# Branch B's meta keys: four heads packed into one transposed block, evacuated onto the diagonal of one operand

## The chip, the cores and the metric

The kernel runs on one core of a Trainium2 chip. The metric is the device time of one execution in microseconds (us); several executions are timed and their median is given. PE is TensorE, DVE is VectorE, ACT is ScalarE, POOL is GpSimd, SP is SyncE, which here issues the DMAs. L12 is line 12 of the kernel. Lines of the kernel before are used unless a text says otherwise.

## The reference

One encoder block on a sequence of 1024 tokens with width 1024, with 16 learned meta tokens set in front: RMS norm, one projection, two attention branches side by side, sigmoid gates, an output product, a SwiGLU feed-forward of width 2816, and a final norm. All in float32. Branch A is differential attention of 4 heads over all keys. Branch B is the one that changes: 8 query heads in 2 key-value groups, head width 64. A block of 128 queries sees the key block before it, its own, the one after it (keys at most 128 away), and always the 16 meta keys, which carry no distance bias. A sink logit joins the softmax's denominator.

```python
kpos = jnp.concatenate([meta_pos, N_META + win_idx], axis=1)
bias = -slopes[None, :, :, None, None] * dist[:, None, None]
s = jnp.einsum('bnqgrd,bnkgd->bngrqk', q, k).astype(jnp.float32) * scale + bias
m = jnp.maximum(jnp.max(s, axis=-1, keepdims=True), sink_b)
p = jnp.exp(s - m)
denom = jnp.sum(p, axis=-1, keepdims=True) + jnp.exp(sink_b - m)
return jnp.einsum('bngrqk,bnkgd->bnqgrd', (p / denom).astype(v.dtype), v)
```

## The kernel before

**Precision.** A float32 factor is split into a high part (ACT copy into the matmul format fp32r) and a low part (DVE or POOL subtracts the high part). A projection sums three products, high times high, high times low and low times high. For P·V in branch B, V's high and low parts lie side by side in the 128 columns of `vb`, and P's two parts are two moving operands.

**Stages.** Tokens are normed and transposed into `hT_hi` and `hT_lo`. Branch B's group 0 is projected and attended while branch A's heads 0 and 1 are projected (L646 to L652); then group 1's queries are projected (L681) and its units run with the projection of branch A's heads 2 and 3 (L693 to L700). Then come the first gate products (L710 to L721) and branch A's attention with more gate products between, the output product and the feed-forward.

**A unit.** `attend_b` (L316) does one tile of 128 queries for the four heads of one group; with 2 groups and 8 tiles there are 16 units. Its first part makes the scores on PE (`bps`, L331), adds the bias and takes the row minimum on DVE (L333), exponentiates on ACT (L337) with the sink beside it (L339), sums and inverts on DVE (L340, L341) and scales the probabilities `bs` on POOL (L343). POOL then copies the 16 meta columns of each head, twice, into `bmd` (L347), of which two zeroed buffers exist (L271 to L274); the two copies are for the high and the low part of the operand. The second part, `finish()`, goes block by block through the two or three key blocks and, as block 8, the meta keys: four transposes per block into one PSUM bank `bpt` (L356, two buffers), an ACT copy to the high part of `btr` (L358), a DVE subtract to the low part (L360; for the meta block only on 16 rows, over the first of its two copies) and the product with V into the bank `bpy` (L362). At the end ACT and DVE add the halves of `bpy` (L365, L366) and SP stores them. `units_b` (L564) keeps at most one unit open behind the one that starts; in group 1 it calls `sums_of` after each first part, which makes weight sums `gs` on POOL (L608 to L611) and stores them (`ws_d`, L613).

**V.** `project_v` (L240) makes V transposed back in three steps, which `project` calls between its matmuls; the last one is the meta tokens, 32 rows, written into block 8 of a `vb` that is zeroed otherwise (L273, L284).

**Order.** On PE, ACT, DVE and SP a scheduler that estimates a timeline sets the order of the instructions (L68); each engine then runs its row in order and waits on semaphores. POOL's row is written by hand from L678 to L726: it is the order of the code. In it, after the last unit, stand the zeroing of `av`, `as` and `dist_m` (L672, L704, L705) with eight copies into `dist_m` (L708), then the low part `wl_c` of the third pair of gate weights (L118, called from L721; those of the first two pairs are made on DVE, L196), then the low parts of the first two operands `w_gop` of the later gate products (L725, L118). `close_bpool` at L694 gives the memory of branch B's tiles away, and `dist_m` lies where some of them were. The first gate products are six banks `pg_0` to `pg_5` of 12 matmuls each (L717), two for each of the three pairs. The loads `w_g` of the operands `w_gop` (L624) go into buffers that weight sums used before.

Of the kernel before, what the change touches and what calls it, by code (L numbers as in the profile page):

```python
# [9 lines left out]
F32 = mybir.dt.float32  # L10
F32R = mybir.dt.float32r
BF16 = mybir.dt.bfloat16  # L12
I32 = mybir.dt.int32
AF = mybir.ActivationFunctionType
ALU = mybir.AluOpType
# [4 lines left out]
P = 128  # L20
S = 1024
D = 1024
NM = 16
L = S + NM
# [49 lines left out]
def encoder_block(ctx: ExitStack, tc: tile.TileContext, x, meta, norm_mix, w_in, lq1, lk1, lq2, lk2,  # L74
                  subln, sink, w_ba, w_bb, w_o, norm_ffn, w_g, w_u, w_d, norm_final, out, dbg=None):
    nc = tc.nc
# [5 lines left out]
    def f32(ap):  # L82
        return ap.bitcast(F32)

    def pool(name, side="left", space=None, bufs=1):
        kw = {} if space is None else {"space": space}
        if space is not DRAM:
            kw["reuse_waits"] = "tile"
        cm = tc.tile_pool(name=name, bufs=bufs, side=side, **kw)
        p = cm.__enter__()  # L90
        return p, lambda: cm.__exit__(None, None, None)
# [5 lines left out]
    def bank(p, tag, name, bufs):  # L97
        return p.tile([P, 512], F32, tag=tag, name=name, bufs=bufs)
# [10 lines left out]
    ident = const.tile([P, P], F32, name="ident")  # L109
# [48 lines left out]
    psum1, close_psum1 = pool("psum1", space=PSUM)  # L158

    def pp_bank(name):  # L160
        return bank(psum1, "pp", name, 3 if psum1 is not psum2 else PP2)
# [58 lines left out]
    def project(col, chunks, name, evac):  # L220
        ensure(1)
        for i, _ in enumerate(project_steps(col, chunks, name, evac)):
            if i % DC == V_AT and turning_v:
                next(turning_v[0], None)
        ensure(W_BUFS - 1)
# [14 lines left out]
    def project_v(col, name, evac):  # L240
        vt = vtpool.tile([P, L + NM], F32, tag="vt", name=f"vt_{name}", bufs=1)
        project(col, K_CHUNKS, name, lambda ps, at, n: nc.scalar.copy(vt[:, at:at + n], ps))
        nc.vector.tensor_copy(vt[:, L:L + NM], vt[:, S:L])

        def turn():
            for b in range(3):
                nb = 4 if b < 2 else 1
                kp = P if b < 2 else 2 * NM
                pt = pp_bank(f"pv_{name}_{b}").rearrange("p (c t) -> p c t", c=4)
                for i in range(nb):  # L250
                    k = 4 * b + i
                    nc.tensor.transpose(pt[:kp, i, :], vt[:, k * P:k * P + kp], ident)
                evac(pt[:kp, :nb, :], 4 * b, nb, kp)
                yield

        turning_v[:] = [turn()]
# [11 lines left out]
    bpool, close_bpool = pool("bpool")  # L268
    kb = [(bpool if g else lowpool).tile([P, 2, NT, 144], F32R, tag=("k1", "kb")[g], name=f"kb{g}", bufs=1) for g in range(BG)]
    vb = [(bpool if g else vtpool).tile([P, 9, P], F32R, tag=("q1", "vb")[g], name=f"vb{g}", bufs=1) for g in range(BG)]  # L270
    mds = [bpool.tile([P, 4, P], F32, name=f"bmd{i}") for i in range(2)]  # L271
    for i in range(2):
        nc.gpsimd.memset(f32(vb[i])[:, 8, :], 0.0)  # L273
        nc.gpsimd.memset(mds[i], 0.0)  # L274

    def kb_consume(st, at, n):
        b0, nb = at // P, n // P
# [38 lines left out]
    def attend_b(g, t, qb):  # L316
        nm = f"{g}_{t}"
        b0, b1 = max(t - 1, 0), min(t + 2, NT)
        nb = b1 - b0
        W = nb * 144  # L320
        j0 = b0 - t + 1
        tb = tbx[:, j0:j0 + nb, :].rearrange("p j k -> p (j k)")
        st = bpool.tile([P, 4, 432], F32, tag="bs", name=f"bs_{nm}", bufs=2)
        mn = small.tile([P, 4], F32, tag="bmn", name=f"bmn_{nm}")
        dn = small.tile([P, 4], F32, tag="bdn", name=f"bdn_{nm}")
        es = small.tile([P, 4], F32, tag="bes", name=f"bes_{nm}")
        hs = slice(4 * g, 4 * g + 4)
        for r in range(4):
            ps = bank(psum1, "bs", f"bps_{nm}_{r}", 2)
            for v in range(2):  # L330
                nc.tensor.matmul(ps[:, :W], qb[:, r, t * P:(t + 1) * P],  # L331
                                 kb[g][:, v, b0:b1, :].rearrange("p b k -> p (b k)"), start=(v == 0), stop=(v == 1))
            nc.vector.tensor_tensor_reduce(st[:, r, :W], ps[:, :W], tb, 2.0 ** -(4 * g + r + 1), nsink[:, 4 * g + r:4 * g + r + 1],  # L333
                                           ALU.add, ALU.min, mn[:, r:r + 1])
        nc.vector.tensor_tensor(es, mn, sinkb[:, hs], ALU.add)
        for r in range(4):
            nc.scalar.activation(st[:, r, :W], st[:, r, :W], AF.Exp, bias=mn[:, r:r + 1], scale=-1.0,  # L337
                                 accum_out=dn[:, r:r + 1])
        nc.scalar.activation(es, es, AF.Exp)  # L339
        nc.vector.tensor_tensor(dn, dn, es, ALU.add)  # L340
        nc.vector.reciprocal(dn, dn)  # L341
        for r in range(4):
            nc.gpsimd.tensor_scalar(st[:, r, :W], st[:, r, :W], dn[:, r:r + 1], 1.0, ALU.mult, ALU.mult)  # L343

        md = mds[t % 2]
        own = (t - b0) * 144 + P
        nc.gpsimd.tensor_copy(md[:, :, 0:2 * NM].rearrange("p r (a k) -> p r a k", a=2),  # L347
                              st[:, :, own:own + NM].unsqueeze(2).broadcast_to([P, 4, 2, NM]))

        def finish():  # L350
            py = bank(psum1, "by", f"bpy_{nm}", 1)
            blocks = [(k, P, (k - b0) * 144) for k in range(b0, b1)] + [(8, P, (t - b0) * 144 + P)]
            for k, kp, o in blocks:
                pt = bank(psum1, "bt", f"bpt_{nm}_{k}", 2).rearrange("p (r t) -> p r t", r=4)
                for r in range(4):
                    nc.tensor.transpose(pt[:kp, r, :], st[:, r, o:o + P] if k < 8 else md[:, r], ident)  # L356
                tr = bpool.tile([P, 2, 4, P], F32R, tag="btr", name=f"btr_{nm}_{k}", bufs=4)
                nc.scalar.activation(tr[:kp, 0], pt[:kp], AF.Copy)  # L358
                lo = tr[:, 1] if k < 8 else tr[:NM, 0]
                nc.vector.tensor_tensor(lo, pt[:lo.shape[0]], f32(tr[:lo.shape[0], 0]), ALU.subtract)  # L360
                for hl in range(2 if k < 8 else 1):
                    nc.tensor.matmul(py, vb[g][:kp, k, :], tr[:kp, hl].rearrange("p r t -> p (r t)"),  # L362
                                     start=(k == b0 and hl == 0), stop=(k == 8))
            y1 = bpool.tile([64, 512], F32, tag="by1", name=f"by1_{nm}", bufs=2)
            nc.scalar.copy(y1, py[64:128])  # L365
            nc.vector.tensor_tensor(y1, py[0:64], y1, ALU.add)  # L366
            nc.sync.dma_start(yb_d[g][:, t * P:(t + 1) * P].rearrange("(r p) s -> p r s", p=64),
                              y1.rearrange("p (r s) -> p r s", r=4))
        return finish
# [130 lines left out]


    first_b = [attend_b(0, t, qb) for t in range(2)]
    project_v(C_VB, "vb", vb_evac)
    flush_v()
    def quad(hl, kh, half):
# [58 lines left out]
    def units_b(g, qb, pending=(), extra=lambda t: None):  # L564
        pending = list(pending)
        for t in range(len(pending), NT):
            if len(pending) > 1:
                pending.pop(0)()
            pending.append(attend_b(g, t, qb))
            extra(t)  # L570
            if len(pending) > 1:
                pending.pop(0)()
        for p in pending:
            p()
# [135 lines left out]
    for k in range(0, 6, 2):  # L710
        ensure(1)
        wh, wl = prepped.pop((k, k + 1))
        for i in range(2):
# [4 lines left out]
            st = f32(stage.tile([P, 2, 512], F32R, tag="qk", name="gate_first", bufs=QK_BUFS))[:, 0]  # L718
# [41 lines left out]
    psum1 = psum2  # L760
# [130 lines left out]
    for n in range(AH * NT + T_LAG):  # L891
        scoring, turning = iter(()), iter(())
        if n < AH * NT:
            h, t = divmod(n, NT)
# [386 lines left out]
    st = {}  # L1281
# [161 lines left out]
    for n in range(nf, len(steps)):  # L1443
        p, j = steps[n][1]
# [3 lines left out]
        if p in LOADS:  # L1448
            at, half, col = LOADS[p]
            if at <= j < at + 4:  # L1450
                t, cols = 4 * half + j - at, slice(col * 512, col * 512 + 512)
# [60 lines left out]
```

## Time and profile before

| | us |
|---|---|
| median of 3 runs | 1451.38 |
| the runs | 1447.25 to 1451.52 |
| the profiled execution | 1446.1 |
| its span (first to last instruction) | 1444.3 |
| PE busy | 1422.8 |
| POOL busy | 641.3 |
| branch B's transposes L356, first and last start | 78.2 and 303.7 |

In a row of a group or a timeline stands the start and the duration (or, in a group, the count and busy time, then the mean of one in ns), the engine, the line, the operation, and output<-inputs with the buffers' numbers left out. A bracket at the end tells how long the engine was idle before and what released it. Matmuls overlap: the duration of one is longer than the distance to the next. In a row of windows stand start and end, the length, the busy time of PE, of its weight loads (PEld), DVE, ACT and POOL, the granted clock of PE, the DMA share and GB/s.

### The profile page before, as it was taken

To read this page: it belongs to the slowest core of one execution; us is meant where nothing else is said; L and a number is where in the kernel's file an instruction comes from. 1 tells how busy PE (TensorE), PEld (TensorE's weight loads), DVE (VectorE), ACT (ScalarE), POOL (GpSimd) and SP (SyncE) were. 2 spreads that over 40 slices of the span, in tenths; PEclk is the share of its full clock that TensorE was granted. 3 is DMA by queue.
4 is the path that set the end of the run, shared out by engine and by line. 5 is a ranking of instruction groups with operands and counts; after the bars stand their busy time and mean duration, and the time that the engine had idled before them with its cause. 6 is when DMAs were issued, how large, how long until landed. Compare 5 with 4: busy or idle time off the path is not lost.

```text
span 1444.3 us, 21160 instructions
## 1 busy us (share of the span) xinstructions
PE 1422.8 (99%) x7279; PEld 1221.2 (85%) x7279; DVE 899.2 (62%) x1624; ACT 679.6 (47%) x1290; POOL 641.3 (44%) x605
## 2 busy tenths in 40 slices
PE   8999999999999999999999999999999999999997
PEld 6988989988898999888888878888888888888886
DVE  7478536637697989624614966554555553787567
ACT  6366535545665656544413643333333333444454
POOL 5599127743333333334522665544544452000444
PEclk9999999999999999999999999999999999999999
DMA  8467658986557473576612534333332332964443
GB/s 244 90 209 237 193 162 265 288 281 213 190 169 257 147 227 125 190 256 209 216 34 88 152 104 161 109 102 110 102 102 96 110 102 102 331 208 140 124 129 139
DMA packets 188891, 242.41 MB, mean 168 GB/s; under 512 B 18208, under 2 KB 115936, under 8 KB 188784
## 3 DMA queue, kind: packets, MB, share of 16 engines
q1 hardware_dynamic: 188784, 241.07, 52.6%
q8 instruction: 57, 0.93, 0.3%
q14 instruction: 50, 0.41, 0.1%
HBM read 157.45 MB, written 77.00 MB: 162 GB/s over the span
## 4 chain that ended last, share of the span: by engine, by line
PE 81%; POOL 6%; DVE 5%; issue 4%; DMA 2%; ACT 1%; POOLq 0%; SPq 0%; DVEq 0%; ACTq 0%
PE pg L1293 28%; PE pd L1387 9%; PE pg L737 7%; PE po L1070 6%; PE ppa L780 6%; PE aps L796 3%; PE pp_qb L214 3%; POOL oa L118 3%; PE apy L835 3%; PE pp_ka L214 2%; PE pp_va L214 2%; PE apt L822 2%; PE pp_qa L214 2%; PE bpt L356 1%; PE bpy L362 1%
## 5 line engine op out<-in xcount | busy, mean ns | idle before, releaser
L118 POOL TENSOR_TENSOR wop<-wf,wop 128x512 fp32r<-128x512 f32 x128 | 172.6, 1353 | 165.5 <-ACT wop L117 149.6
L1293 PE MATMUL pg<-t,wop 128*128 128x512 f32 x1056 | 242.6, 389 | 0.0
L1293 PEld LDWEIGHTS pg<-t,wop 128*128 128x128 f32 x1056 | 198.3, 188 | 41.1
L1387 PE MATMUL pd<-ob,oa 128*128 128x512 f32 x924 | 209.9, 389 | 0.4 <-POOL oa L118 0.4
L1387 PEld LDWEIGHTS pd<-ob,oa 128*128 128x128 f32 x924 | 173.4, 188 | 36.8 <-POOL oa L118 0.8
L1293 PE MATMUL pg<-b,wop 128*128 128x512 f32 x792 | 185.6, 392 | 2.3 <-DVE c L1302 2.3
L1293 PEld LDWEIGHTS pg<-b,wop 128*128 128x128 f32 x792 | 149.5, 189 | 34.1 <-issue 2.4
L737 PE MATMUL pg<-hT_hi,gop 128*128 128x512 f32 x384 | 142.7, 396 | 0.0
L118 POOL TENSOR_TENSOR oa<-ra,oa 128x512 fp32r<-128x512 f32 x33 | 44.0, 1335 | 170.1 <-ACT oa L117 168.6
L117 ACT ACTIVATE wop<-wf 128x512 fp32r<-128x512 f32 x128 | 80.2, 631 | 82.9 <-PE pg L1293 48.6
L118 POOL TENSOR_TENSOR gop<-gr,gop 128x512 fp32r<-128x512 f32 x48 | 63.3, 1319 | 116.4 <-ACT gop L117 102.6
L117 ACT ACTIVATE oa<-ra 128x512 fp32r<-128x512 f32 x77 | 48.7, 632 | 105.9 <-PE pd L1387 45.1
L804 ACT ACTIVATE as<-as,amn 128x1040 f32<-128x1040 f32 x64 | 74.5, 1164 | 46.9 <-DVE amn L799 42.8
L1128 DVE TENSOR_TENSOR s<-wf,wf 128x512 f32<-128x512 f32 x22 | 25.0, 1138 | 108.1 <-DMA wf<-in_w_ff_gate_dram 58.0
L796 PE MATMUL aps<-ak,aq 128*128 128x392 f32 (+1 forms) x384 | 90.0, 330 | 1.3 <-DVE amn L799 0.6
L1070 PE MATMUL po<-woh,mT 128*128 128x512 f32 x384 | 88.0, 390 | 0.0
L1070 PEld LDWEIGHTS po<-woh,mT 128*128 128x128 f32 x384 | 71.9, 188 | 14.8
L796 PEld LDWEIGHTS aps<-ak,aq 128*128 128x128 f32 x384 | 69.6, 189 | 15.0 <-DVE amn L799 2.2
L737 PEld LDWEIGHTS pg<-hT_hi,gop 128*128 128x128 f32 x384 | 72.7, 189 | 11.2 <-DVE gk L742 0.2
L343 POOL TENSOR_SCALAR bs<-bs,bdn 128x432 f32<-128x432 f32 (+1 forms) x64 | 41.4, 666 | 85.5 <-DVE bdn L341 73.4
L737 PE MATMUL pg<-hT_lo,gop 128*128 128x512 f32 x192 | 76.0, 396 | 0.0
L807 POOL TENSOR_SCALAR as<-as,adn,neglam 128x1040 f32<-128x1040 f32 x32 | 38.8, 1214 | 62.5 <-DVE adn L805 43.9
(287 smaller groups left out, 3099.0 us busy)
## 6 DMA issues: line engine op xcount, KB each, us to landing
ra<-aop SPq DMA_DIRECT2D x77, 256.0 KB, 2.6
wf<-in_w_ff_gate_dram SPq DMA_DIRECT2D x24, 512.0 KB, 4.0
wf<-in_w_ff_up_dram SPq DMA_DIRECT2D x24, 512.0 KB, 3.9
aop<-as SPq DMA_DIRECT2D x44, 256.0 KB, 2.1
w_c<-in_w_in_dram SPq DMA_DIRECT2D x17, 512.0 KB, 5.7
aop<-c SPq DMA_DIRECT2D x33, 256.0 KB, 2.0
ts_d<-to SPq DMA_DIRECT2D x16, 512.0 KB, 3.7
gw<-in_w_in_dram SPq DMA_DIRECT2D x32, 256.0 KB, 3.9
```

The source lines that it names most:

```text
L117: nc.scalar.activation(hi, src, AF.Copy)
L118: lo_eng.tensor_tensor(lo, src, f32(hi), ALU.subtract)
L214: nc.tensor.matmul(ps[:, :n], a[:, c, :], b[:, c, at:at + n], start=(c == 0 and i == 0), stop=(c == DC - 1 and i == 2))
L343: nc.gpsimd.tensor_scalar(st[:, r, :W], st[:, r, :W], dn[:, r:r + 1], 1.0, ALU.mult, ALU.mult)
L737: nc.tensor.matmul(ps, op[:, a, c], quad(b, *act)[:, c], start=(p in (2, 5, 1) and c == 0 and i == 0), stop=(p in (2, 3, 4) and c == 3 and ...
L780: nc.tensor.matmul(ps, w[:, a, j, :], src(j, b, tk), start=(j == 0 and n == 0), stop=(j == 3 and n == 2))
L796: nc.tensor.matmul(ps[:, :n], qs[m][:, t * P:(t + 1) * P], ks[m][:, vv, k0:k0 + n], start=(vv == 0), stop=(vv == 1))
L804: nc.scalar.activation(s[m][:, 0:L], s[m][:, 0:L], AF.Exp, bias=low, scale=-1.0, accum_out=dn[:, m:m + 1])
L835: nc.tensor.matmul(py[:, cols], v[:kp, a, k, :], at_[:kp, k, b, :], start=(k == 0 and j == 0), stop=(k == 8))
L1070: nc.tensor.matmul(ps, mT[:, c, a, t * P:(t + 1) * P], wos[q, c][:, b], start=(c == 0 and n == 0), stop=(c == DC - 1 and n == 2))
L1293: nc.tensor.matmul(ps, op[:, x, c, :], b[:, y, c, :], start=(p in (1, 2, 5) and c == 0 and n == 0), stop=(p in (4, 2, 3) and c == 3 and n ...
L1387: nc.tensor.matmul(ps[u], oa[:, a, u * P:(u + 1) * P], ob[:, b, :], start=(p in (1, 2, 5) and j == 0 and k == 0), stop=(p in (2, 3, 4) and ...
```

## The change

The zeroed buffers `bmd` go; the packed copy is now 128 columns without gaps, 4 heads times 2 copies times 16 keys. One transpose in place of four turns it, and stands first in `finish()`, ahead of the tile's other blocks. Its 128 rows are then written, 32 rows a head, by four pairs of an ACT copy and a DVE subtract, onto the diagonal blocks of one operand `diag` that is zeroed once. Block 8 of `vb` holds the meta tokens' V eight times, so that every row of `diag` meets the right V row; its product is the last of the tile.

```diff
+        meta = vt[:, S:S + 2 * NM]
+        if name == "vb":
+            meta = bpool.tile([P, P], F32, tag="by1", name="vb_meta", bufs=2)
+            nc.vector.tensor_copy(meta.rearrange("p (a k) -> p a k", a=8), vt[:, S:L].unsqueeze(1).broadcast_to([P, 8, NM]))
...
-    mds = [bpool.tile([P, 4, P], F32, name=f"bmd{i}") for i in range(2)]
-    for i in range(2):
-        nc.gpsimd.memset(f32(vb[i])[:, 8, :], 0.0)
-        nc.gpsimd.memset(mds[i], 0.0)
+    diag = bpool.tile([P, 4, P], F32R, name="diag")
+    nc.gpsimd.memset(f32(diag), 0.0)
...
-        md = mds[t % 2]
+        md = bpool.tile([P, 4, 2, NM], F32, tag="bmd", name=f"bmd_{nm}", bufs=2)
         own = (t - b0) * 144 + P
-        nc.gpsimd.tensor_copy(md[:, :, 0:2 * NM].rearrange("p r (a k) -> p r a k", a=2),
-                              st[:, :, own:own + NM].unsqueeze(2).broadcast_to([P, 4, 2, NM]))
+        nc.gpsimd.tensor_copy(md, st[:, :, own:own + NM].unsqueeze(2).broadcast_to([P, 4, 2, NM]))
 
         def finish():
             py = bank(psum1, "by", f"bpy_{nm}", 1)
-            blocks = [(k, P, (k - b0) * 144) for k in range(b0, b1)] + [(8, P, (t - b0) * 144 + P)]
-            for k, kp, o in blocks:
+            pt = bank(psum1, "bt", f"bpt_{nm}_8", 2)[:, 0:P]
+            nc.tensor.transpose(pt, md.rearrange("p r a k -> p (r a k)"), ident)
+            for r in range(4):
+                hi, lo = slice(32 * r, 32 * r + 32), slice(32 * r, 32 * r + NM)
+                nc.scalar.activation(diag[hi, r], pt[hi], AF.Copy)
+                nc.vector.tensor_tensor(diag[lo, r], pt[lo], f32(diag[lo, r]), ALU.subtract)
+            for k in range(b0, b1):
+                o = (k - b0) * 144
...
+                    nc.tensor.matmul(py, vb[g][:, k, :], tr[:, hl].rearrange("p r t -> p (r t)"),
+                                     start=(k == b0 and hl == 0), stop=False)
+            nc.tensor.matmul(py, vb[g][:, 8, :], diag.rearrange("p r t -> p (r t)"), start=False, stop=True)
```

In the kernel after, the packed transpose is L355, the ACT copy onto the diagonal L358, the other transposes L364, their copies L366, the products L369 and L371, the gate products L725, the zeroing of `dist_m` L713.

PE's row where unit 7 of group 1 ends, in the kernel before (`bpy_7` is that unit's output bank, `btr_7_6` to `btr_7_8` its blocks, `pg_0` and `pg_1` the first gate products):

```order
L717 MATMUL pg_0_3748<-hT_hi,wh_c_3724 128x512
L717 MATMUL pg_0_3748<-hT_lo,wh_c_3724 128x512
L362 MATMUL bpy_7_3142<-btr_7_6_3148,vb_149 128x512 x2
L362 MATMUL bpy_7_3142<-btr_7_7_3158,vb_149 128x512 x2
L717 MATMUL pg_0_3748<-hT_hi,wl_c_3725 128x512
```

The meta block's product of unit 7 follows when 17 of the 72 matmuls of L717 have stood. The same place in the kernel after:

```order
L364 MATMUL bpt_6_6_3161<-ident,bs_6_2988 128x128 x4
L364 MATMUL bpt_6_7_3171<-ident,bs_6_2988 128x128 x4
L369 MATMUL bpy_6_3140<-btr_6_6_3166,vb_149 128x512 x2
L355 MATMUL bpt_7_8_3187<-ident,bmd_7_3122 128x128
L369 MATMUL bpy_6_3140<-btr_6_7_3176,vb_149 128x512 x2
L371 MATMUL bpy_6_3140<-diag,vb_149 128x512
L364 MATMUL bpt_7_6_3197<-ident,bs_7_3090 128x128 x4
L369 MATMUL bpy_7_3186<-btr_7_6_3202,vb_149 128x512 x2
L364 MATMUL bpt_7_7_3207<-ident,bs_7_3090 128x128 x4
L369 MATMUL bpy_7_3186<-btr_7_7_3212,vb_149 128x512 x2
L371 MATMUL bpy_7_3186<-diag,vb_149 128x512
L725 MATMUL pg_4_3872<-hT_hi,wl_c_3869 128x512
```

Units 6 and 7 now stand together behind 52 of the 72 gate matmuls, and the matmul behind them is the first that reads `wl_c` of the third pair.

ACT's row at the end of unit 7, in the kernel before (`wh_c` and `w_gop` are high parts of gate weights):

```order
L358 ACTIVATE btr_7_7_3158<-bpt_7_7_3153 128x512
L556 ACTIVATE va_stage<-pv_va_2_3695 32x128
L358 ACTIVATE btr_7_8_3168<-bpt_7_8_3163 128x512
L117 ACTIVATE wh_c_3783<-w_c_3780 128x1024
L232 ACTIVATE qk_stage<-pp_ka_0_3685 128x384
L719 COPY gate_first<-pg_0_3748 128x512
L365 COPY by_1_7_3172<-bpy_7_3142 64x512
L117 ACTIVATE w_gop_3860<-w_g_3858 128x512
```

And after:

```order
L373 COPY by_1_6_3182<-bpy_6_3140 64x512
L358 ACTIVATE diag<-bpt_7_8_3187 32x128
L366 ACTIVATE btr_7_6_3202<-bpt_7_6_3197 128x512
L358 ACTIVATE diag<-bpt_7_8_3187 32x128 x2
L117 ACTIVATE w_gop_3906<-w_g_3904 128x512
L358 ACTIVATE diag<-bpt_7_8_3187 32x128
L366 ACTIVATE btr_7_7_3212<-bpt_7_7_3207 128x512
```

The first `w_gop` copy, which stood behind the unit's output, stands between its third and fourth copy onto the diagonal. POOL's row around `dist_m` is the same in both.

More of the change, by code (lines that the diff above doesn't have):

```diff
@@ L247, in turn @@
                 nb = 4 if b < 2 else 1
-                kp = P if b < 2 else 2 * NM
+                kp = P if b < 2 else meta.shape[1]
                 pt = pp_bank(f"pv_{name}_{b}").rearrange("p (c t) -> p c t", c=4)
@@ L251, in turn @@
                     k = 4 * b + i
-                    nc.tensor.transpose(pt[:kp, i, :], vt[:, k * P:k * P + kp], ident)
+                    nc.tensor.transpose(pt[:kp, i, :], vt[:, k * P:k * P + kp] if b < 2 else meta, ident)
                 evac(pt[:kp, :nb, :], 4 * b, nb, kp)
@@ L354, in finish @@
+            for k in range(b0, b1):
+                o = (k - b0) * 144
                 pt = bank(psum1, "bt", f"bpt_{nm}_{k}", 2).rearrange("p (r t) -> p r t", r=4)
                 for r in range(4):
-                    nc.tensor.transpose(pt[:kp, r, :], st[:, r, o:o + P] if k < 8 else md[:, r], ident)
+                    nc.tensor.transpose(pt[:, r, :], st[:, r, o:o + P], ident)
                 tr = bpool.tile([P, 2, 4, P], F32R, tag="btr", name=f"btr_{nm}_{k}", bufs=4)
-                nc.scalar.activation(tr[:kp, 0], pt[:kp], AF.Copy)
@@ L359, in finish @@
[L359 to L363, printed above, removed]
+                nc.scalar.activation(tr[:, 0], pt, AF.Copy)
+                nc.vector.tensor_tensor(tr[:, 1], pt, f32(tr[:, 0]), ALU.subtract)
@@ L364, in finish @@
+                for hl in range(2):
+                    nc.tensor.matmul(py, vb[g][:, k, :], tr[:, hl].rearrange("p r t -> p (r t)"),
+                                     start=(k == b0 and hl == 0), stop=False)
+            nc.tensor.matmul(py, vb[g][:, 8, :], diag.rearrange("p r t -> p (r t)"), start=False, stop=True)
             y1 = bpool.tile([64, 512], F32, tag="by1", name=f"by1_{nm}", bufs=2)
```

## The prediction

> **What bounds the kernel now.** I read the page first, then the busy time by windows over the stretch that the change touches, then each engine's timeline in the tail of group 1.
>
> ```profile
> span 1444.3 us, 21160 instructions
> PE 1422.8 (99%) x7279; PEld 1221.2 (85%) x7279; DVE 899.2 (62%) x1624; ACT 679.6 (47%) x1290; POOL 641.3 (44%) x605
> PE 81%; POOL 6%; DVE 5%; issue 4%; DMA 2%; ACT 1%; POOLq 0%; SPq 0%; DVEq 0%; ACTq 0%
> 288.00:309.90 21.90, 21.90 (x137) 20.21 (x137) 12.64 (x25) 10.37 (x22) 9.24 (x16) 1.00 0.89 288
> 309.90:320.00 10.10, 10.10 (x45) 8.20 (x44) 0.68 (x1) 5.03 (x8) 7.74 (x12) 1.00 0.90 245
> ```
>
> TensorE (PE) is 99% busy and holds 81% of the chain that ended last. The last two rows (start and end, length, then busy time of PE, PEld, DVE, ACT and POOL, the clock, the DMA share, GB/s) show the tail of group 1: PE is full, at full clock, and the other four have room. So a transpose less is time less there, as long as PE's next instruction is always ready. And whatever PE waits for, in its fixed order, comes out one for one.
>
> **What is removed.** Three of four transposes per tile, 16 tiles: 48.
>
> ```profile
> L356 PE MATMUL bpt<-ident,bmd 128*128 128x128 f32 x64 | 10.4, 272 | 0.0
> 257.58 0.60 PE L356 MATMUL bpt<-ident,bmd 128*128 128x128 f32 x4
> 257.93 0.47 PE L214 MATMUL pp_qa<-hT_hi,wh_c 128*128 128x512 f32 x1
> 258.25 0.39 PE L214 MATMUL pp_qa<-hT_lo,wh_c 128*128 128x512 f32 x1
> 258.47 0.39 PE L214 MATMUL pp_qa<-hT_hi,wl_c 128*128 128x512 f32 x1
> ```
>
> The 272 ns of the first row is a latency; the stream shows the price. Four transposes start at 257.58, the next matmul 0.35 us later, and the one after it 0.32 later, where matmuls of this size otherwise follow at 0.22 (258.25 to 258.47). So four cost 0.35 + 0.10 = 0.45, one about 0.11, and 48 cost 48 x 0.11 = **5.2 us**. By the latency it would be 10.4 x 48/64 = 7.8, which I keep as the other end; the starts are the nearer evidence, since PE overlaps. The matmul on the operand stays one per tile.
>
> The zeroing on POOL at the program's start shrinks and one DVE broadcast copy for the V operand comes in. I cost both at nothing: POOL has 2.4 us free in the second window and far more before the first tile, DVE over 9 of 21.9 us in the first. Without that cover they are under 1 us.
>
> **What is added per tile.** The single ACT copy of 128x512 and DVE subtract of 16x512 become four pairs on a single `diag`. In the built program each ACT copy waits for the DVE subtract before it, so it is a ladder of eight steps, and the first copy of a tile waits for the tile before's matmul on `diag`. Nearest rows:
>
> ```profile
> 301.49 0.60 ACT L358 ACTIVATE btr<-bpt 128x512 fp32r<-128x512 f32 x1
> 302.12 0.27 ACT L556 ACTIVATE va_stage<-pv_va 32x128 fp32r<-32x128 f32 x1
> 302.12 0.69 DVE L360 TENSOR_TENSOR btr<-bpt,btr 128x512 fp32r<-128x512 f32 x1
> 302.73 0.27 DVE L557 TENSOR_TENSOR va_stage<-pv_va,va_stage 32x128 fp32r<-32x128 f32 x1
> ```
>
> The 32x128 rows have nearly the shapes of a ladder step: 0.27 on ACT, 0.27 on DVE, with about 0.06 to hand over 0.6 a pair, 2.4 us a tile, against 0.60 + 0.69 before. In the body of the two groups this lies beside projections. It can still reach PE, because the block's PSUM bank (one of two) is held until the fourth subtract. For that I take 0.6 us in all, out of 0 to 3: not below 0, since PE had no idle there to win, and 3 if about 10 of the 16 tiles pay 0.3.
>
> **What is moved.** This term decides. The scheduler, seeing a longer ladder, put the units of group 1 later in PE's row. Before, the last PV matmul of unit 7 stood after 17 of the 72 gate matmuls of L717. Now all of units 6 and 7 stand back to back behind 52 of them, and the next gate matmul is the first that takes `wl_c` of the third weight pair. That low part is made by POOL, whose order is written by hand:
>
> ```profile
> 309.87 0.39 PE L362 MATMUL bpy<-btr,vb 128*128 128x512 f32 x1
> 318.21 0.39 PE L717 MATMUL pg<-hT_hi,wl_c 128*128 128x512 f32 x1
> 310.32 0.20 POOL L705 MEMSET dist_m<- 128x128 f32 x1 [1.58 <-PE bpy L362]
> 310.47 2.69 POOL L708 COPY dist_m<-dist 128x240 f32<-128x240 f32 x8
> 313.95 2.41 POOL L118 TENSOR_TENSOR wl_c<-w_c,wh_c 128x1024 fp32r<-128x1024 f32 x1 [0.79 <-ACT wh_c L117]
> 316.30 2.55 POOL L118 TENSOR_TENSOR w_gop<-w_g,w_gop 128x512 fp32r<-128x512 f32 x2
> ```
>
> `dist_m` takes over pool memory that unit 7 used, so its memset waits for unit 7's last PV matmul. Before, that ended at 310.26 and the low part was done at 316.36, 1.85 us before PE wanted it at 318.21: hidden. Now PE wants it directly behind unit 7: memset 0.20, copies 2.69, split 2.41 = **5.3 us** in which PE has nothing to do, whatever happens earlier.
>
> Earlier there is the end of the units themselves, which before had projections and gate matmuls to cover it and now has none. I follow it from T0, the end of unit 7's last score matmul.
>
> ```profile
> 289.21 0.51 DVE L333 CUSTOM_DVE_ANT_0 bs<-bps,tbx,nsink 128x288 f32<-128x288 f32 x1
> 290.85 0.53 ACT L337 ACTIVATE bs<-bs,bmn 128x288 f32<-128x288 f32 x1
> 291.84 0.20 ACT L339 ACTIVATE bes<-bes 128x4 f32<-128x4 f32 x1
> 292.59 0.15 DVE L340 TENSOR_TENSOR bdn<-bdn,bes 128x4 f32<-128x4 f32 x1
> 292.78 0.18 DVE L341 RECIPROCAL bdn<-bdn 128x4 f32<-128x4 f32 x1
> 311.09 0.58 ACT L365 COPY by<-bpy 64x512 f32<-64x512 f32 x1
> 311.71 0.68 DVE L366 TENSOR_TENSOR by<-bpy,by 64x512 f32<-64x512 f32 x1 [3.28 <-ACT by L365]
> 293.15 1.94 POOL L343 TENSOR_SCALAR bs<-bs,bdn 128x288 f32<-128x288 f32 x4 [6.39 <-DVE bdn L341]
> 295.16 0.29 POOL L347 COPY bmd<-bs 128x128 f32<-128x128 f32 x1
> 295.41 0.72 POOL L608 TENSOR_TENSOR gs<-gw 128x256 f32<-128x256 f32 x1
> 297.61 0.74 POOL L611 TENSOR_TENSOR gs<-gw,gs 128x256 f32<-128x256 f32 x1
> ws_d<-gs SPq DMA_DIRECT2D x1, 256.0 KB, 2.8
> w_g<-in_w_in_dram SPq DMA_DIRECT2D x2, 256.0 KB, 3.5
> 312.29 0.63 ACT L117 ACTIVATE w_gop<-w_g 128x512 fp32r<-128x512 f32 x1 [0.62 <-DMA w_g<-in_w_in_dram]
> ```
>
> Reduction 0.51, exponential 0.53, sink 0.20, sum and reciprocal 0.33, with accumulator reads and hand-overs about 2.0. In that time unit 5 ends, its output goes out (0.58 ACT, 0.68 DVE, to 3.0), and unit 6's ladder (2.4) ends at 5.4. Its last two blocks (transposes, 0.60 + 0.69 each, partly beside one another) come to 7.4, its PV matmuls to 8.1, its output to 9.4. Three pairs of unit 7's ladder end at 11.2.
>
> Now ACT's row has, between the third and fourth copy of unit 7's ladder, the copy that splits the first gate weight (`w_gop0`). Its load `w_g0` goes into a buffer that a weight-sum tile of k = 7 has to leave first. POOL scales unit 7 (1.94) and packs (0.29) to about 4.3, and makes four sums at 0.71 (295.41 to 298.35 for four) to 7.15. The store takes 2.8 and the load behind it 3.5 from issue: 13.5, with SP's issuing about 14.0. ACT stands until then: copy 0.63, fourth pair 0.6 to 15.2, the last block to 16.2, unit 7's PV matmuls to **16.9**. With 5.3 behind it PE resumes at 22.3. PE's own work in that time is 16 matmuls at 0.23 and 21 transposes at 0.11, 6.0 us. The stall is 22.3 - 6.0 = **16.3 us**.
>
> Bounds of it: if the load is early, the chain without that wait ends at 13.8 and the stall is 13. If the units keep up after all, the forced 5.3 alone is left. If the store waits in the queues (a DMA share of 0.90), each doubling adds 3 to 6: 22.
>
> **The clock.**
>
> ```profile
> 336.00:338.00 2.00, 0.09 (x1) 0.00 (x0) 1.77 (x5) 2.00 (x6) 0.33 (x1) 1.00 1.05 409
> 338.00:340.00 2.00, 1.97 (x11) 1.88 (x12) 1.85 (x9) 1.68 (x5) 1.29 (x2) 0.66 1.05 407
> 340.00:342.00 2.00, 2.00 (x7) 1.71 (x6) 1.94 (x6) 1.40 (x4) 1.17 (x1) 0.50 1.07 408
> 342.00:344.00 2.00, 2.00 (x11) 1.72 (x11) 1.71 (x3) 0.00 (x0) 0.00 (x0) 0.98 0.86 322
> ```
>
> An idle PE in 336 to 338 was followed by a granted clock of 0.66 and 0.50 for 4 us: 2 x 0.34 + 2 x 0.50 = 1.7 lost. The same after the long stall: +1.7, and about 0.5 on PE's short steps inside it.
>
> The Trainium skill, "TensorE: Matmul & The Clock Gate", section "Part 1: The HAM clock gate (the "warmup" mystery)", has the clock halve after at least one idle window of about 3.4 us and return after as much sustained work. Here under 2 us of idle sufficed, so the row decides on the first half; the return after 3 to 4 us agrees. By the rule the short gaps inside the ladders would cost no clock and the sum would be up to 0.5 less.
>
> **The sum.** -5.2 + 16.3 + 0.5 + 1.7 + 0.6 = +13.9, about **+14 us**. The profiled execution took 1446.1 (span 1444.3), so 1460; the median of the runs shown, 1451.4, stands 5.3 above that execution, so 1465 by it. I take 1463.
>
> **The rivals.** (1) The load of `w_g0` is early. POOL's sums stand in a fixed order behind unit 7's scaling, which speaks against it. Stall 13, sum +11, 1457 to 1462. (2) The units keep up and only the forced 5.3 is left: -5.2 + 5.3 + 1.7 + 0.6, +2.4, 1448 to 1454. For it: before, ACT and DVE had over half of that stretch free. Against: the ladder is bound by hand-overs, not by their load. (3) The other side, faster: PE's arrival at the third pair's low part. If PE comes there 5.3 us or more after unit 7's last PV matmul, because its queue is late for another reason such as the weight load of that pair, the forced wait is hidden and the 48 transposes stay won: -5.2, 1441 to 1446. Against it is the order itself, in which nothing stands between the two. (4) The chain is longer: the store or the load takes twice as long, or the ladder stalls PE by the full 3 us in the body. Sum up to +22, 1468 to 1474.
>
> **How the numbers follow.** Forecast 0.50, (1) 0.18, (2) 0.10, (3) 0.05, (4) 0.17. A measurement of this kernel can tell about 0.3%, 4.4 us, from no change. Faster by more than that: case (3), 0.05. Within it: most of (2), 0.08. Slower: the rest, 0.87. The range 1453 to 1475 holds the forecast, (1), the upper edge of (2) and nearly all of (4), and leaves out some 0.17.
>
> **What would show it.** In the profile after: L355 with 16 transposes in place of 64 on `bmd`; PE idle of over 10 us in one place around 310 to 335, its last piece released by POOL's `wl_c` (L118), the pieces before it by ACT and DVE of `diag`; POOL waiting at the `dist_m` memset (L713) for PE's L371; ACT waiting for the `w_g` load between two `diag` copies; the clock under 0.7 after the stall. Elsewhere PE keeps 99%. I am wrong if PE shows no wait at `wl_c` (then case (3)), if the units' last PV matmul ends within 10 us of T0 (then (1) or (2)), or if new PE idle stands in the earlier tiles, which I costed at 0.6.

## The result and the profile after

| | before | after |
|---|---|---|
| median, us | 1451.21 (4 runs, 1447.25 to 1451.52) | 1462.74 (4 runs, 1460.15 to 1463.65) |
| profiled execution, us | 1446.1 | 1462.05 |
| its span, us | 1444.3 | 1460.2 |
| PE busy, us | 1422.8 | 1423.6 |

The ratio after to before is 1.0083, with a 95% interval of 1.0061 to 1.0105: slower by 8.9 to 15.2 us, where 12 to 14 was forecast. PE is busy for as long as before and idle for 36.6 us in place of 21.5. The page of the kernel after, and the larger of PE's waits between 60 and 345 us (total, times, longest):

```profile
span 1460.2 us, 21109 instructions
PE 1423.6 (97%) x7231; PEld 1217.5 (83%) x7231; DVE 909.9 (62%) x1673; ACT 689.0 (47%) x1338; POOL 640.2 (44%) x602
```

```profile
PE bpy L369 <- ACT btr L366: 6.1, 3, 3.1
PE pg L725 <- POOL wl_c L118: 5.3, 1, 5.3
PE bps L334 <- DVE bmn L336: 0.9, 2, 0.6
PE bpt L364 <- DVE diag L359: 0.6, 1, 0.6
```

Before, from 60 us up to the same point of its row, PE waited 0.2 for `btr` and otherwise only here:

```profile
PE bps L331 <- DVE bmn L333: 1.0, 3, 0.5
```

Nearly all the new waiting is in one place, the end of group 1. PE's timeline there:

```profile
307.70 0.43 PE L334 MATMUL bps<-kb,qb 128*128 128x288 f32 x2
...
311.52 0.47 PE L369 MATMUL bpy<-btr,vb 128*128 128x512 f32 x1 [2.02 <-ACT btr L366]
...
318.07 0.47 PE L369 MATMUL bpy<-btr,vb 128*128 128x512 f32 x1 [1.04 <-ACT btr L366]
...
322.78 1.52 PE L369 MATMUL bpy<-btr,vb 128*128 128x512 f32 x2 [3.07 <-ACT btr L366]
324.10 0.63 PE L371 MATMUL bpy<-diag,vb 128*128 128x512 f32 x1
330.00 0.80 PE L725 MATMUL pg<-hT_hi,wl_c 128*128 128x512 f32 x1 [5.27 <-POOL wl_c L118]
...
337.11 0.39 PE L745 MATMUL pg<-hT_hi,w_gop 128*128 128x512 f32 x1
```

Unit 7's last score ends at 308.13, its last product at 324.73, and PE resumes at 330.00. `T0` below is the end of that last score, as in the prediction. ACT and POOL show why:

```profile
319.06 0.27 ACT L358 ACTIVATE diag<-bpt 32x128 fp32r<-32x128 f32 x1 [0.64 <-DVE diag L359]
321.18 0.63 ACT L117 ACTIVATE w_gop<-w_g 128x512 fp32r<-128x512 f32 x1 [1.85 <-DMA w_g<-in_w_in_dram]
321.84 0.27 ACT L358 ACTIVATE diag<-bpt 32x128 fp32r<-32x128 f32 x1
322.13 0.60 ACT L366 ACTIVATE btr<-bpt 128x512 fp32r<-128x512 f32 x1
```

```profile
324.79 0.20 POOL L713 MEMSET dist_m<- 128x128 f32 x1 [5.74 <-PE bpy L371]
324.94 2.70 POOL L716 COPY dist_m<-dist 128x240 f32<-128x240 f32 x8
327.59 2.35 POOL L118 TENSOR_TENSOR wl_c<-w_c,wh_c 128x1024 fp32r<-128x1024 f32 x1
```

The split of the gate weight (`w_gop`) stands in the ladder and waits for its load; POOL starts `dist_m` the moment unit 7 ends, and the low part follows. The first later gate product, which is the same instruction in both kernels, is a good mark: 337.11 here, and in the kernel before

```profile
322.88 0.39 PE L737 MATMUL pg<-hT_hi,w_gop 128*128 128x512 f32 x1
```

So 14.2 of the 15.9 us between the spans are there at the end of the changed stretch; the rest comes in branch A. This first later gate product is called the mark below. From it on, PE's row holds the same instructions in the same order in the kernel before, the kernel after and every run below whose trace is read. PE's clock in the stall:

```profile
310.00:315.00 5.00, 2.49 (x12) 1.59 (x13) 3.38 (x9) 3.30 (x9) 4.21 (x8) 1.00 0.65 217
315.00:320.00 5.00, 3.23 (x15) 1.87 (x14) 2.74 (x6) 1.94 (x6) 3.97 (x9) 1.00 0.56 182
320.00:325.00 5.00, 1.95 (x3) 0.79 (x3) 0.99 (x2) 2.36 (x5) 0.21 (x2) 0.65 0.56 159
325.00:330.00 5.00, 0.01 (x1) 0.01 (x1) 0.68 (x1) 0.35 (x1) 5.00 (x10) 0.50 0.49 134
330.00:334.00 4.00, 4.00 (x9) 3.13 (x10) 0.00 (x0) 0.00 (x0) 2.40 (x2) 0.50 0.73 268
334.00:336.00 2.00, 2.00 (x8) 1.61 (x7) 0.00 (x0) 0.59 (x1) 0.00 (x0) 0.71 0.01 4
```

### The profile page after: what moved, and what is told of

It is laid out like the page before. It is cut to its first block, busy times and chain, and to the rows that moved or that the text cites. A ratio compares the mean times of both kernels' runs of the same rounds, so it can differ in the third digit from the quotient of the medians.

```text
span 1460.2 us, 21109 instructions
## 1 busy us (share of the span) xinstructions
PE 1423.6 (97%) x7231; PEld 1217.5 (83%) x7231; DVE 909.9 (62%) x1673; ACT 689.0 (47%) x1338; POOL 640.2 (44%) x602
## 4 chain that ended last, share of the span: by engine, by line
PE 64%; issue 4%; POOL 4%; DVE 3%; DMA 2%; ACT 1%; POOLq 0%; DVEq 0%; ACTq 0%; SPq 0%
PE pg L1301 27%; PE pd L1395 9%; PE pg L745 7%; PE ppa L788 6%; PE po L1078 6%; PE aps L804 3%; PE apy L843 3%; POOL oa L118 3%; PE apt L830 2%; DMA g_d<-gk 1%; DMA gk<-g_d 1%; DVE t L118 1%; DVE as L807 1%; DVE as L818 1%; PE pg L725 0%
```

## The experiments

The theory on test: the 48 transposes save 5.2 us, and the order of the rows loses more, because units 6 and 7 end late in PE's row with POOL's `dist_m` and `wl_c` behind them. Rivals: the small copies cost by themselves; the block's place ahead of the others does it alone; POOL's order does it alone. The runs were timed in three groups, each beside its own runs of the kernel before; "above" and "below" are against those.

**POOL's order, in the kernel after.**

```diff
-    nc.gpsimd.memset(dist_m[:, :, S - last_k0:], 0.0)
-    for t in range(NT): ... (the eight copies)
...
     for n in range(2):
         g_load(n, ...)
         g_split(n, ...)
+    nc.gpsimd.memset(dist_m[:, :, S - last_k0:], 0.0)
+    for t in range(NT): ... (the eight copies)
```

> The kernel after, with the zeroing of dist_m and its eight copies moved behind the last w_gop split in POOL's hand-written row; PE's row stays the same. Theory (units 6 and 7 late in PE's row, then POOL's wl_c behind dist_m): PE's last wait of 5.3 us at wl_c goes and with it about 1 us of low clock, the 7 us of waits inside the units stay: 1456, 1454 to 1458. Rival 1 (the longer chain of small copies costs by itself and the wl_c wait only hides behind something else that is late): 1461 to 1463. Rival 2 (POOL's order is the whole loss): 1446 to 1449.

Measured: median 1460.08 against 1448.39, ratio 1.0077 (1.0059 to 1.0096), outside the 1454 to 1458 expected. In its profiled execution (1456.5) PE's wait at `wl_c` is gone and the mark comes 8.3 us earlier than after, at 328.84. But then, in the PE and ACT timelines of this run:

```profile
337.76 0.49 PE L745 MATMUL pg<-hT_hi,gop 128*128 128x512 f32 x1 [0.94 <-ACT gop L117]
```

```profile
337.08 0.63 ACT L117 ACTIVATE gop<-gr 128x512 fp32r<-128x512 f32 x1 [4.62 <-DMA gr<-ws_d]
```

PE comes early and waits for the next gate operand, whose load has not landed, and later 1.7 for a minimum of branch A's first tiles. The wait at `wl_c` was real and 5.3 us long, but others stood close behind it. The profile kept 5.5 of the 8.3 us; the medians, which spread in two groups (1455.7 to 1457.4 and 1462.8 to 1463.8), show at most a few.

**The same move in the kernel before.** The same edit.

> The kernel before with the same move in POOL's row. Theory: before, wl_c was ready 1.85 us ahead of PE, so nothing changes: 1451, 1449 to 1453. Rival (dist_m later makes branch A's first tile late): 1453 to 1455.

Measured: 1449.32 against 1448.39, ratio 1.0000 (0.9992 to 1.0009). Before, POOL's order cost nothing, as its 1.85 us of slack had said.

**Short ladder, block last.** The four copies first, then the four subtracts; the block behind the key blocks.

```diff
+            pt = bank(psum1, "bt", f"bpt_{nm}_8", 2)[:, 0:P]      (now behind the loop over k)
+            nc.tensor.transpose(pt, md.rearrange("p r a k -> p (r a k)"), ident)
             for r in range(4):
                 nc.scalar.activation(diag[hi, r], pt[hi], AF.Copy)
-                nc.vector.tensor_tensor(diag[lo, r], pt[lo], f32(diag[lo, r]), ALU.subtract)
+            for r in range(4):
+                lo = slice(32 * r, 32 * r + NM)
+                nc.vector.tensor_tensor(diag[lo, r], pt[lo], f32(diag[lo, r]), ALU.subtract)
```

> The kernel after with the four ACT copies first and the four DVE subtracts behind them (no hand-over between the pairs), and the packed block as the last one of the tile as it was before. The built row has unit 7's last product behind 33 of the 72 gate matmuls, 19 ahead of the first that needs wl_c. Theory (the ladder at the head of each unit is what made the units late): the 48 transposes stay saved, the waits inside the units nearly go, 19 matmuls (4.4 us) cover most of POOL's 5.3: 1448, 1445 to 1451. Rival 1 (64 more small instructions on ACT and DVE cost time wherever they stand): 1458 or more.

Measured: 1450.79 against 1448.39, ratio 1.0016 (1.0005 to 1.0027). The long stall is gone, so the small copies do not cost 10 us wherever they stand. But the saving is not there either. The PE, DVE and ACT timelines of this run:

```profile
310.30 0.39 PE L373 MATMUL bpy<-diag,vb 128*128 128x512 f32 x1
...
321.04 0.39 PE L747 MATMUL pg<-hT_hi,w_gop 128*128 128x512 f32 x1
...
331.41 0.59 PE L747 MATMUL pg<-hT_hi,gop 128*128 128x512 f32 x1 [2.39 <-ACT gop L117]
```

```profile
305.86 1.24 DVE L372 TENSOR_TENSOR diag<-bpt,diag 16x128 fp32r<-16x128 f32 x4 [0.47 <-ACT diag L369]
```

```profile
313.92 0.63 ACT L117 ACTIVATE w_gop<-w_g 128x512 fp32r<-128x512 f32 x1 [2.53 <-DMA w_g<-in_w_in_dram]
314.57 0.58 ACT L375 COPY by<-bpy 64x512 f32<-64x512 f32 x1
...
330.73 0.63 ACT L117 ACTIVATE gop<-gr 128x512 fp32r<-128x512 f32 x1 [6.07 <-DMA gr<-ws_d]
```

Unit 7's last product starts at 310.30, no earlier than before (309.87). It is not the unit's chain that holds it: the last subtract into `diag` ends at 307.10, and PE does not wait for it. PE's row has this product behind 33 gate products, where 17 stood ahead of it before, and PE comes to it 3.2 us after its operand is complete. In the kernel before it came 4.6 us after:

```profile
304.61 0.68 DVE L360 TENSOR_TENSOR btr<-bpt,btr 16x512 fp32r<-16x512 f32 x1 [1.61 <-ACT btr L358]
```

So the order that the scheduler chose sets the end of the unit in both. A row with the product further ahead was not tried. Up to the mark PE is busy for 311.7 us, where it was 315.6 before, and idle for 9.3, where it was 7.3: the mark comes 1.8 us earlier. Behind the mark 4.3 us are lost against before, 2.4 of them in the wait for the operand's load.

**The same with POOL's order too.** Both edits.

> The run with the short ladder as the last block and dist_m behind the splits in POOL's row. Theory: no wait at wl_c is left, only the saving of 5.2 us stays: 1446, 1444 to 1448. Rival 1 (small instructions cost by themselves): 1456 or more.

Measured: 1450.36 against 1448.39, ratio 1.0008 (0.9998 to 1.0018): 4 us above what was expected. The run with the short ladder had no wait at `wl_c` left for this move to take, and PE again waits for `gop` (1.2 for ACT's part, 0.7 for POOL's).

**The price of a transpose.** In the kernel before, the meta block's four transposes issued twice.

```diff
-                for r in range(4):
+                for r in [0, 1, 2, 3] * (2 if k == 8 else 1):
```

> The kernel before with the meta block's four transposes issued twice into the same bank (64 more, the same data). If a transpose in the stream costs 0.11 us, as read from the starts, 64 cost 7.0 us: 7 above the kernel before of this call, 6 to 8. If its latency of 0.27 us counts: 17 above. If PE's time there is partly covered by what branch A's start waits for (POOL's splits and the loads of the next operands): 2 to 5 above.

Measured: ratio 1.0053 (1.0039 to 1.0068), 7.7 us above 1448.84 (5.7 to 9.9), or 0.12 each for 64. Its profiled execution took 8.2 ms and is not used. The price of 0.11 holds for transposes added; a price of 0.27, the latency, is refuted, and so is the cover that would have left 2 to 5 us.

**ACT's order, in the kernel after.** The `w_gop` copies on ACT are kept behind unit 7's output copy; `last_out` holds that copy.

```diff
-            nc.scalar.copy(y1, py[64:128])
+            last_out[:] = [nc.scalar.copy(y1, py[64:128])]
...
+        with tc.issue_after(last_out[0].ins):
             g_split(n, ...)
```

> The kernel after; on ACT alone, the w_gop copies are kept behind the output copy of unit 7 (they stood between the third and fourth copy of its ladder). PE's row is the same. If ACT's wait for the w_g load delays unit 7 as forecast, PE's wait of 3.1 us ahead of unit 7's last products shrinks by about 2.3, and all behind it comes 2 to 3 us earlier: 9 to 10 above the kernel before (the kernel after stood 11.5 above). Rival (another hand-over is late in its place): no change, 11 to 12 above.

Measured: 1460.48 against 1448.84, ratio 1.0085 (1.0072 to 1.0098), 12.3 above where 9 to 10 was expected. In the profile the wait of 3.1 is down to 0.9, unit 7's last product starts 2.5 us earlier (321.6 for 324.1; 0.8 of it were there at `T0`) and the mark stands at 334.17, 2.9 earlier; the span is 1458.0, 2.2 shorter. The medians can't tell it from the kernel after (1.0083, and 1.0095 when that was timed again). That the wait depends on ACT's order is shown; a gain in time is not.

**ACT's order, with the short ladder last.** The same edit on the short ladder.

> The run with the short ladder as the last block, and the w_gop copies behind unit 7's output copy on ACT. If branch A's first loads start from unit 7's stored output (it was stored at 316.2 there, at 312.4 before) and these set when the next gate operand is ready, PE's wait of 2.4 us for it goes: 0 to 1 above the kernel before, in place of 2.4 above. If the landing of the 1 MB load of av alone sets it: no change, 2 to 3 above. If the saved transposes count in full: 4 to 5 below.

Measured: 1447.28 against 1448.84, ratio 0.9991 (0.9981 to 1.0002). Against the run without it (1.0016) this is some 3.6 us. The output copy of unit 7 comes at 310.88 for 314.57, and the next operand's split on ACT at 328.59 for 330.73. PE's wait of 2.4 for it is gone, and with it a low clock: from 330 to 336 the clock is 1.00 here, where it was 0.71 and 0.73 in the run without it. What remains of PE's new waits between 60 and 420 us is

```profile
PE pg L729 <- ACT gate_first L731: 1.6, 1, 1.6
PE bpy L375 <- DVE diag L374: 0.9, 1, 0.9
PE apt L835 <- DVE as L824: 0.7, 1, 0.7
PE pg L750 <- POOL gop L118: 0.6, 1, 0.6
```

**Long ladder, block last.** The block moved behind the loop; the pairs stay as in the kernel after.

> The kernel after with the packed block moved back to the end of the tile; the ladder keeps its hand-overs. In the built row unit 7's last product again stands behind 52 of the gate matmuls, right ahead of the one that needs wl_c, but units 5 and 6 stand earlier. If the forced wait behind unit 7 is what counts, it shows about 5 us of it and 1 to 3 us of waits inside the units: 5 to 8 above the kernel before. If the position of the block alone made the loss: 0 to 3 above. If the ladder alone did: 11 above.

Measured: 1454.71 against 1448.84, ratio 1.0045 (1.0033 to 1.0057), 6.5 above. PE's largest new waits in it:

```profile
PE pg L725 <- POOL wl_c L118: 5.3, 1, 5.3
PE bpy L371 <- DVE diag L370: 2.2, 1, 2.2
PE pg L725 <- DVE qk_stage L233: 1.5, 1, 1.5
```

The forced wait behind unit 7 is there in full, and the unit ends at 318.5 in place of 324.7.

**The kernel after again**, for the last group of runs.

> The kernel after, unchanged, as the yardstick beside the other three of this call: 10 to 13 above the kernel before. If its loss were a matter of the chip: another size.

Measured: 1461.98 against 1449.15, ratio 1.0095 (1.0082 to 1.0108).

**Short ladder, block first.** The four copies ahead of the four subtracts, nothing else.

> The kernel after with the four copies ahead of the four subtracts, the packed block first in the tile as in the kernel after: the fourth corner beside the long ladder last (6.5 above) and the short ladder last (2.4 above). In the built row unit 7 again ends right ahead of the matmul that needs wl_c. If that place sets the size: the wait of 5.3 and 1 to 3 inside the units, 6 to 9 above the kernel before. If the hand-overs of the ladder alone made the loss: 2 to 3 above. If the block's place ahead of the others alone made it: 11 above.

Measured: 1457.43 against 1449.15, ratio 1.0065 (1.0049 to 1.0082), 9.4 above where 6 to 9 was expected, with the same wait of 5.3 at `wl_c` and one of 2.3 where ACT's `w_gop` copy waits for its load inside unit 7. With it the four corners are complete (us above the kernel before, ratio less one times its median; in brackets the start of unit 7's last product and the gate products ahead of it in PE's row):

| | block first | block last |
|---|---|---|
| pairs handed over one by one | 13.8 (324.1, 52) | 6.5 (318.0, 52) |
| copies, then subtracts | 9.4 (318.5, 52) | 2.3 (310.3, 33) |

The place is worth 7.1 to 7.3, the hand-overs 4.2 to 4.4, and they add, with each corner known to some 2 us. The scheduler made each corner's row anew, so these are prices of the rows that it built and not of the chains alone. Neither of the two alone made the loss.

**Both moves in the kernel after.** POOL's and ACT's edits together.

> The kernel after with both moves: dist_m behind the splits on POOL and the w_gop copies behind unit 7's output on ACT; PE's row is that of the kernel after. At the first later gate product PE should stand some 10 us earlier than the kernel after. If nothing else is late, 1 to 2 above the kernel before. If branch A's start waits instead for its loads, which start from unit 7's end (322 here, 310 before): 6 to 9 above, with PE's new waits on gop and on the first tiles' minimum.

Measured: 1456.33 against 1449.15, ratio 1.0052 (1.0035 to 1.0069), 7.5 above; the kernel after stood 13.8 above in this group. The mark did not come 10 us earlier in the profiled execution: 335.62. Its trace holds another event, told in the last section, which leaves PE 5.6 us behind at `T0` (313.73 for 308.13). From `T0` the mark comes after 21.9 us; in the kernel after it takes 29.0, with POOL's move alone 22.1. So ACT's move adds next to nothing to POOL's here: unit 7's last product starts 1.4 us sooner after `T0`, but from it to the mark the clock is 0.65, where it was 0.80 with POOL's move alone. Behind the mark PE waits 1.6 for the first tiles' minimum, but not at `gop`, and the 1 MB load of `av` is issued at 331.7, behind unit 7's stored output. PE's row is the same as after, so some 6 us of the loss lay in the rows of POOL and ACT. How the 7.5 that remain are shared between the order of PE's row, what starts from unit 7's end and events like that one was not separated.

**ACT's order once more.** The short ladder last, and `w_gop` behind the fourth output copy of the first gate products.

> The short ladder as the last block, with the w_gop copies on ACT behind the fourth output copy of the first gate products (in the run with w_gop only behind unit 7's output, the gate product waited 1.6 us for an output copy that stood behind w_gop). If that wait goes and nothing takes its place: 2 to 3 below the kernel before. If the loads of the next operands bound branch A's start there: 0 to 1.5 below, with PE's wait at gop in its place.

Measured: 1448.2 against 1449.15, ratio 0.9996 (0.9986 to 1.0005). The wait for `gate_first` is gone; PE waits 0.9 at `wl_c` and 2.7 for `gop` in its place. No version of this study is faster than the kernel before beyond its interval.

## Why the prediction was right, and where it was not

- **The place and the chain: right.** From the end of unit 7's scores, 16.9 was forecast for the end of its products and 22.3 for PE's return; the trace has 16.6 and 21.9 (16.9 and 5.3 make 22.2). The forced piece was put at 5.3 and is 5.27. ACT waits for the `w_g` load between the third and fourth copy, as followed. Part of the agreement is luck: the load let ACT go on after 13.1 us where 14.0 was followed, and the last three products took 1.95 us, at a clock of 0.65, where 0.7 was taken.
- **The stall: right.** 21.9 less the 6.0 us at which the prediction priced PE's own work is 15.9, for 16.3 forecast. In the trace PE is idle for 12.8 of the 21.9 and busy for 9.0, 3.0 more than that price: transposes and products take longer in short runs between waits, at a mean clock of 0.81, than in a full stream.
- **The clock: half right.** The long stall was followed by 0.50 from 330 to 334 and 0.71 to 336, a loss of 2.6 where 1.7 was taken. But the short gaps cost nothing before the last two: after waits of 2.02 and 1.04 the rows from 310 to 320 have 1.00. The 0.5 for them was wrong up to the wait of 3.07. Before, 1.94 us of idle were followed by half clock, so the length of a gap alone does not decide it here; PE's busy share of a fixed stretch of 3.41 us does, as the last section works out. The Trainium skill ("TensorE: Matmul & The Clock Gate", section "Part 1: The HAM clock gate (the "warmup" mystery)") ties the drop to an idle window of about 3.4 us. That length agrees with the traces; but in the stretches ahead of the two drops PE was not idle throughout, it was busy for 1.47 us (before) and 1.38 us (after).
- **What the ladder does in the body: taken too high.** 0.6 was taken. PE's one wait on `diag` (0.6, at 313.79) stands in the tail and is part of the 21.9; up to 305 the ladder makes no wait of PE. In the run with both moves it did, for 3.4 and 0.5 us (last section).
- **The sum at the mark: right.** +13.9 forecast, +14.2 measured. The terms do not all fit so well (the clock 2.6 for 1.7, the ladder in the body nothing for 0.6), and some of their errors cancel. The profiled executions differ by 16.0, the medians by 11.5 and, timed again, 12.8; 1463 was forecast and 1462.74 measured. The level of the kernel before changed between the groups of runs (1448.4 to 1451.2), and part of so close an agreement is luck.
- **Why the units came late: incomplete.** The prediction had the longer ladder as the scheduler's reason. By the four corners both count. In time the place of the block ahead of the others weighs more, 7 to 4; in the start of unit 7's last product they weigh about alike (6 to 8 us each). That a block which stands first puts its chain ahead of every other block's evacuation, and as the last one runs beside them, would fit; why the scheduler answers so was not looked into.
- **The saving as a term of its own: wrong.** The sum took -5.2 as won in any case, and rival (3) gave 1441 to 1446 if the stall were hidden. With the stall gone (short ladder last) the time is 1.0016 and 1.0008 of before, and 0.9991 and 0.9996 with ACT's order mended. PE's transposes do cost 0.12 each when added. Taking them away did not bring unit 7's end forward, because the scheduler put more gate products ahead of its last product (33 for 17), 3.2 us after the operand was complete; and branch A's first products wait for loads and splits that come behind that end. The step that failed is "PE is full, so a transpose less is time less there": it held only as long as the next engine's work was ready, and at the mark at most 1.8 us of the 5.2 were left.

That the next operand is late because its load is late is shown by the waits named at `gop<-gr`. That this load in turn is held by unit 7's output is suggested, not shown: with the short ladder last, ACT's move let SP store that output 3.9 us earlier (312.27 for 316.21) and the loads `gr` began 2.2 us earlier (325.43 for 327.64), but it moved other copies of ACT as well.

## What to carry to other kernels

A busy engine's saved work was worth no more here than the slack of what came next: look, behind the stretch that is shortened, for the first wait of the other engines, and see what it starts from. When a step is split into small pairs, count the hand-overs and the buffers held through them, and try the longest chain at the end of the unit as well as at its head; here the end was 7 us better. When a scheduler sets the rows, read the rows: see how long an operand has been ready when the engine comes to it, and whether saved time has only moved other work ahead; and what follows the delayed step on the engines with a fixed order (here POOL's) told the stall to within a microsecond.

## What the runs showed of the hardware

In the run with both moves, one DVE subtract of 128x512 took 7.28 us; of the sixteen of its kind in the kernel before the median is 1.08 and the longest 2.22. Its DVE, PE and POOL timelines:

```profile
85.85 7.28 DVE L118 TENSOR_TENSOR to<-ta,to 128x512 fp32r<-128x512 f32 x1 [0.43 <-ACT to L117]
93.16 0.30 DVE L361 TENSOR_TENSOR diag<-bpt,diag 16x128 fp32r<-16x128 f32 x1
```

```profile
93.61 0.30 PE L357 MATMUL bpt<-ident,bmd 128*128 128x128 f32 x1 [3.37 <-DVE diag L361]
```

```profile
85.11 2.41 POOL L118 TENSOR_TENSOR wl_c<-w_c,wh_c 128x1024 fp32r<-128x1024 f32 x1
87.48 0.28 POOL L352 COPY bmd<-bs 128x128 f32<-128x128 f32 x1
87.73 1.31 POOL L541 TENSOR_TENSOR ta<-hT_lo 128x512 f32<-128x512 f32 x1
89.00 2.36 POOL L118 TENSOR_TENSOR wl_c<-w_c,wh_c 128x1024 fp32r<-128x1024 f32 x1
91.33 1.25 POOL L542 TENSOR_TENSOR ta<-ta,ta 128x512 f32<-128x512 f32 x1
```

The subtract reads two operands from SBUF and lasts through five POOL instructions that follow each other without a gap. The fourth `diag` subtract stands behind it on DVE and holds the PSUM bank, so PE waits 3.4 us for it; the clock is 0.64 and 0.51 in the 4 us from 94 on, and at `T0` PE is 5.6 us behind the kernel after. The Trainium skill ("SBUF — State Buffer", section "Who interferes with whom") says that a DVE instruction with two SBUF inputs contends with a GpSimd instruction that reads SBUF, and that the pair of ports they share is an exclusive lock. The rows agree, and show that DVE can lose several times in a row. Whether this makes the two groups of times of the first run with POOL's order, 6 us apart, was not shown: only one execution of each kernel has a trace.

The granted clock follows PE's busy share of fixed stretches. In each of the thirteen traces that are read, all changes of the clock between 1.00 and 0.50 lie a whole number of 3.41 us apart. In the kernel before, PE is busy for 1.47 us from 335.24 to 338.65, and the next 3.41 us have 0.50. In the kernel after, PE is busy for 1.62 us from 307.87 to 311.28, which holds most of the wait of 2.02, and the next stretch has 1.00; it is busy for 1.38 us from 318.11 to 321.52, and the next has 0.50. Over all the traces, every such stretch at full clock with less than 1.48 us of busy time was followed by half clock, and none with more than 2.05; in between it went either way.
